# A decoder layer's feed-forward: w_up's products in 512 columns, and the norm, convolution and silu of most activations in w_down's stage

## The chip, the cores and the metric

The kernel runs on one core of a Trainium2 chip. The metric is the device time of one execution in microseconds (us); less is better. The core has five engines, each with its own instruction queue that it works through in order: TensorE (PE in the profile, its weight loads PEld), VectorE (DVE), ScalarE (ACT), GpSimd (POOL), and SyncE (SP), which here only issues DMAs. They meet through semaphores.

## What is computed

One decoder layer on 512 tokens of width 2048 in float32: a token mixer, a cross-attention, a convolutional feed-forward and a final norm. The change concerns the feed-forward alone (4096 gate and 4096 value features):

```
h = h + conv_ffn(rmsnorm(h, norm_ffn), w_up, ffn_conv, w_down)

def conv_ffn(hn, w_up, ffn_conv, w_down):
    up = causal_dwconv(hn @ w_up, ffn_conv)      # three taps along the tokens
    gate, val = jnp.split(up, 2, axis=-1)
    return (jax.nn.silu(gate) * val) @ w_down

out = rmsnorm(h, norm_final)
```

The scale of the norm that belongs to a token (`rstd`) is a factor of a whole column here, so the kernel multiplies it in after the product with w_up.

## The kernel before

**Numbers in two parts.** Matmuls take float32 operands in a rounded form. To keep precision each operand is split: `wh` is the rounded value (a cast on ACT), `wl` the rest (a subtraction on DVE). A product then needs three matmuls per k: high weights by high features, high weights by low features, low weights by high features.

**w_up's stage** (region `p_g`). Activations are made in 32 pairs j: 128 gate features and 128 value features, for all 512 tokens. The first three pairs (`plain_pair`) are plain products. The other 29 (`up_pair`) use Strassen's scheme in Winograd's form on 2x2 blocks (two halves of the 2048 input features, two halves of the tokens): seven products of 8 k each instead of eight. The token halves are 256 wide (`HT`), and the features of all seven forms lie ready in SBUF as high and low parts side by side (`xb`, `fb`). `product` splits a weight block into the two pool buffers `wh`, `wl` and runs the 24 matmuls of one product into a PSUM tile; `combine` makes the sums of weight blocks on DVE. The weight blocks of a pair come in by four DMAs of 512 KB on SP's queue, into `sraw` (four buffers) and `raw` (three). The sum a21 + a22 is made by a fifth DMA on POOL's queue, which adds while it stores. The PSUM tiles a, b, c, d hold running sums; DVE adds c's copy `s7` (in the small pool `misc`, buffer name `m0`, two buffers), and multiplies by `rstd` into `v`.

`conv_mult` follows at once: for value and gate a scaled copy on ACT and two multiply-adds on DVE (the taps), silu on ACT, gate times value on POOL, and a store of the 128 x 512 activation to DRAM (`a_d[j]`) on POOL's queue.

**w_down's stage** (region `p_d`). The 32 activations are taken in four chunks of eight. For each chunk four groups g of 512 output features follow; a group is 8 k by 4 token tiles by three matmuls of 512 columns, 96 in all. `load_acts` loads a chunk's activations from `a_d` into `m0` and splits them (`ah`, `al`), all eight behind the first group of the chunk before. `down_weights` loads two k of w_down by one DMA into `raw` and splits them into `wh` and `wl`, again two buffers each, so a split waits until PE has used up the pair of k before the last. DVE adds four finished sums to `ht` after each group. In chunk 0 each group is preceded by loads and transposes of the residual (`load_h`). Chunk 3 runs groups 2 and 3 first, then token tile by token tile with the final norm.

**What sets the order.** The scheduler of the tile framework orders each engine's instructions ahead of time, by data, buffers and priority. Weight loads, splits and combinations carry `high_priority(1000000)`. Once built, the order of each engine is fixed.

Of the kernel before, what the change touches and what calls it, by code (L numbers as in the profile page):

```python
# [17 lines left out]
P = 128  # L18
# [40 lines left out]
def decoder_kernel(ctx: ExitStack, tc: tile.TileContext, x, mem, norm_mix, w_in, dn_conv, dn_a_log, dn_dt_bias, dn_norm,  # L59
# [920 lines left out]
    NCH = 4  # L980
    a_d = [dram.tile([P, S], F32, name=f"a{j}") for j in range(32)]
    with region("p_g") as gp:
# [22 lines left out]
        def sums(k):  # L1005
            hg = sp_.tile([P, 2, S], F32, name="sraw", bufs=4)
# [7 lines left out]
            dve.tensor_tensor(v[:, 0, :], b11, b12, op=ALU.subtract)  # L1014
            dve.scalar_tensor_tensor(v[:, 1, :], v[:, 0, :], -1.0, b22, op0=ALU.mult, op1=ALU.subtract)
            dve.tensor_tensor(v[:, 2, :], b22, b12, op=ALU.subtract)
            dve.scalar_tensor_tensor(v[:, 3, :], v[:, 1, :], -1.0, b21, op0=ALU.mult, op1=ALU.subtract)
# [13 lines left out]
        def product(acc, w, of, first):  # L1031
            wh, wl = (wsp.tile([P, 8, P], F32R, name=n) for n in ("wh", "wl"))
            with tc.high_priority(1000000):
                act.copy(wh, w)  # L1034
                dve.tensor_tensor(wl, w, wh.bitcast(F32), op=ALU.subtract)  # L1035
            for k in range(8):
# [3 lines left out]
                pe.matmul(acc, wl[:, k, :], m[:, 0, :], start=False, stop=(k == 7), skip_group_check=True)  # L1040
# [6 lines left out]
        def up_pair(j):  # L1047
            quad = []
            with tc.high_priority(1000000):
                for i, (h, c) in enumerate(((0, j), (0, 32 + j), (1, 32 + j), (1, j))):  # L1050
                    r = rawp.tile([P, 8, P], F32, name="raw") if i % 2 else sp_.tile([P, 8, P], F32, name="sraw", bufs=4)
# [4 lines left out]
            a, b, c, d = (pw.tile([P, HT], F32, name=n) for n in ("sa", "sb", "sc", "sd"))  # L1056
            v, u = two("v"), two("u")
# [10 lines left out]
            s2 = combine(a11, s1, a11, ALU.add)  # L1068
            s7 = misc.tile([P, HT], F32, name="m0")
# [182 lines left out]
```

## Time and profile before

| | us |
|---|---|
| median of 3 runs | 2847.39 |
| lowest, highest | 2843.1, 2848.35 |
| profiled execution | 2842.91 |
| its span | 2841.1 |
| w_up's 29 pairs, first to last matmul | 1879.0 to 2470.4 |
| w_down, first matmul | 2471.3 |

How to read the lines. A row of the groups gives line, engine, operation, what it writes and reads, shape and count; then busy time, the mean of one in ns, the idle time before them and who ended it. A row of the timeline gives start, duration, engine, line and operation; where several like ones are merged, the duration is that of all. A matmul's duration is its latency, which overlaps with the next one's; the distance of starts is what it costs. Starts are counted from the span's beginning. The granted clock of TensorE was full in all the stretches that are shown.

### The profile page before, as it was taken

What the parts mean: (1) busy time and instruction counts of PE and PEld (TensorE: products, weight loads), DVE (VectorE), ACT (ScalarE), POOL (GpSimd) and SP (SyncE); (2) the same over time, 40 slices, a digit from 0 to 9 for tenths busy, and PEclk for the clock granted to TensorE, in tenths of its full rate; (3) what the DMA queues carried; (4) which work ended last, traced back from release to release, by engine and by line L of the source; (5) the groups of instructions that cost most, each with busy time, mean ns of one, the idle gap of its engine ahead of it and who ended that gap; (6) DMA issues with size and microseconds to landing.
All of it is one profiled execution on the core that took longest, in us unless ns stands there. A gap on an engine that the chain in (4) does not pass through costs nothing. (4 is left out here: it accounts for less than half of the span.)

```text
span 2841.1 us, 40771 instructions
## 1 busy us (share of the span) xinstructions
PE 2778.4 (98%) x15959; PEld 2402.4 (85%) x15959; DVE 1851.8 (65%) x2771; ACT 1261.4 (44%) x2099; POOL 349.8 (12%) x317
## 2 busy tenths in 40 slices
PE   7999999999999999999999999999999999999998
PEld 7788888887888877778888887789999999978886
DVE  7777787877777645434554345778888888743435
ACT  6455555545434434443223333644545455532223
POOL 3000000001011000010231110311111111100002
PEclk9999999999999999999999999999999999999999
DMA  6544444443222222223555432766666666553323
GB/s 211 137 133 138 135 133 127 134 127 93 57 67 60 54 69 67 67 71 89 159 173 161 141 119 86 230 165 139 148 139 148 139 147 139 162 172 125 120 97 112
DMA packets 528467, 354.53 MB, mean 125 GB/s; under 512 B 15345, under 2 KB 483810, under 8 KB 527634
## 3 DMA queue, kind: packets, MB, share of 16 engines
q1 hardware_dynamic: 487872, 303.74, 37.3%
q0 software_dynamic: 39760, 47.93, 7.6%
q8 instruction: 125, 2.05, 0.3%
q14 instruction: 68, 0.56, 0.1%
q10 hardware_dynamic: 642, 0.26, 0.0%
HBM read 316.74 MB, written 35.13 MB: 124 GB/s over the span
## 5 line engine op out<-in xcount | busy, mean ns | idle before, releaser
L164 DVE TENSOR_TENSOR wl<-raw,wh 128x512 fp32r<-128x512 f32 x394 | 290.6, 773 | 258.7 <-ACT wh L163 255.7
L170 PE MATMUL acc<-x,wl 128*128 128x512 f32 x1152 | 455.2, 395 | 1.1 <-DVE wl L164 1.1
L168 PE MATMUL acc<-x,wh 128*128 128x512 f32 x1152 | 455.3, 395 | 0.5 <-ACT wh L163 0.5
L169 PE MATMUL acc<-x,wh 128*128 128x512 f32 x1152 | 455.2, 395 | 0.0
L163 ACT CAST wh<-raw 128x512 fp32r<-128x512 f32 x408 | 235.7, 621 | 412.0 <-PE acc L169 208.2
L170 PEld LDWEIGHTS acc<-x,wl 128*128 128x128 f32 x1152 | 217.0, 188 | 47.0 <-DVE wl L164 2.8
L168 PEld LDWEIGHTS acc<-x,wh 128*128 128x128 f32 x1152 | 216.9, 188 | 44.2 <-issue 1.0
L169 PEld LDWEIGHTS acc<-x,wh 128*128 128x128 f32 x1152 | 216.9, 188 | 44.0 <-issue 1.7
L1034 ACT CAST wh<-sraw 128x1024 fp32r<-128x1024 f32 x87 | 91.7, 1054 | 150.0 <-PE sa L1039 93.3
L1169 DVE TENSOR_TENSOR wl<-raw,wh 128x512 fp32r<-128x512 f32 x112 | 72.4, 688 | 131.1 <-ACT wh L1168 131.0
L1168 ACT CAST wh<-raw 128x512 fp32r<-128x512 f32 x112 | 64.1, 620 | 177.6 <-PE gps L1175 171.4
L1034 ACT CAST wh<-raw 128x1024 fp32r<-128x1024 f32 x87 | 91.5, 1052 | 110.7 <-PE sd L1039 58.2
L1040 PE MATMUL sb<-fb,wl 128*128 128x256 f32 x464 | 131.4, 283 | 0.0
L1038 PE MATMUL sa<-x,wh 128*128 128x256 f32 x464 | 131.3, 283 | 0.0
L1039 PE MATMUL sa<-x,wh 128*128 128x256 f32 x464 | 131.3, 283 | 0.0
L1038 PE MATMUL sb<-fb,wh 128*128 128x256 f32 x464 | 131.3, 283 | 0.0
L1040 PE MATMUL sa<-x,wl 128*128 128x256 f32 x464 | 131.3, 283 | 0.0
L1039 PE MATMUL sb<-fb,wh 128*128 128x256 f32 x464 | 131.3, 283 | 0.0
L366 DVE TENSOR_TENSOR wl<-sm,wh 128x1024 fp32r<-128x1024 f32 x67 | 82.1, 1226 | 62.2 <-ACT wh L365 62.2
L1035 DVE TENSOR_TENSOR wl<-sraw,wh 128x1024 fp32r<-128x1024 f32 x87 | 106.3, 1222 | 19.2 <-ACT wh L1034 19.2
L1035 DVE TENSOR_TENSOR wl<-raw,wh 128x1024 fp32r<-128x1024 f32 x87 | 106.1, 1220 | 17.2 <-ACT wh L1034 17.2
L365 ACT CAST wh<-sm 128x1024 fp32r<-128x1024 f32 x67 | 70.6, 1053 | 84.8 <-PE sb L370 28.9
(584 smaller groups left out, 7595.5 us busy)
## 6 DMA issues: line engine op xcount, KB each, us to landing
raw<-in_w_in_dram SPq DMA_DIRECT2D x146, 512.0 KB, 3.8
raw<-in_w_up_dram SPq DMA_DIRECT2D x70, 512.0 KB, 4.9
raw<-in_w_down_dram SPq DMA_DIRECT2D x64, 512.0 KB, 3.8
sraw<-in_w_up_dram SPq DMA_DIRECT2D x58, 512.0 KB, 4.5
sraw<-in_w_in_dram SPq DMA_DIRECT2D x50, 512.0 KB, 3.8
raw<-in_w_o_dram SPq DMA_DIRECT2D x32, 512.0 KB, 4.1
raw<-in_w_up_dram POOLq DMA_DIRECT2D x29, 512.0 KB, 7.0
gate<-g POOLq DMA_DIRECT2D x21, 512.0 KB, 2.9
```

What stands on the lines that cost most here:

```text
L163: act.copy(wh[:, part, :], raw[:, part, :])
L164: (pool if share and s0 else dve).tensor_tensor(wl[:, part, :], raw[:, part, :], wh[:, part, :].bitcast(F32), op=ALU.subtract)
L168: pe.matmul(acc, wh[:, j, :], hs[k], start=(k == 0), stop=False)
L169: pe.matmul(acc, wh[:, j, :], ls[k], start=False, stop=False)
L170: pe.matmul(acc, wl[:, j, :], hs[k], start=False, stop=(k == nk - 1))
L366: dve.tensor_tensor(wl, w, wh.bitcast(F32), op=ALU.subtract)
L1034: act.copy(wh, w)
L1035: dve.tensor_tensor(wl, w, wh.bitcast(F32), op=ALU.subtract)
L1038: pe.matmul(acc, wh[:, k, :], m[:, 0, :], start=(first and k == 0), stop=False, skip_group_check=True)
L1039: pe.matmul(acc, wh[:, k, :], m[:, 1, :], start=False, stop=False, skip_group_check=True)
L1040: pe.matmul(acc, wl[:, k, :], m[:, 0, :], start=False, stop=(k == 7), skip_group_check=True)
L1169: dve.tensor_tensor(wl, raw[:, i, :], wh.bitcast(F32), op=ALU.subtract)
```

## The change

1. `product` writes 512 columns: high weights by high and low features side by side in one matmul of 512 columns (two halves of a PSUM tile twice as wide), then low weights by high features, 256 columns, into the first half. The two halves are added later (the folding): ACT copies one half or DVE adds `s7`, then DVE adds the halves, with `m0` as the place for it; `s7` moves to `sg`.
2. The sum a21 + a22 is made by DVE; the accumulating DMA is gone. Some signs change (in `sums` and `combine`) so that no negation is needed.
3. `up_pair` no longer multiplies by `rstd`, nor runs the convolution: it stores the raw pair `v` (128 x 1024) to DRAM, `up_d[j]`. A new function `late_act` loads it, multiplies by `rstd` on DVE and runs `conv_mult`. For pairs 3 to 7 this is asked for within w_up's stage (behind pairs 12, 15, 18, 21, 24, with one buffer `cv`), for pairs 8 to 31 in w_down's stage (two buffers `cv` and `cu`), three activations behind each of the first three groups, with the split straight from `cu`.
4. `sraw` has three buffers instead of four.

```diff
             for k in range(8):
                 m = of(k)
-                pe.matmul(acc, wh[:, k, :], m[:, 0, :], start=(first and k == 0), stop=False, skip_group_check=True)
-                pe.matmul(acc, wh[:, k, :], m[:, 1, :], start=False, stop=False, skip_group_check=True)
-                pe.matmul(acc, wl[:, k, :], m[:, 0, :], start=False, stop=(k == 7), skip_group_check=True)
+                pe.matmul(av, wh[:, k, :], m, start=(first and k == 0), stop=False, skip_group_check=True)
+                pe.matmul(av[:, 0, :], wl[:, k, :], m[:, 0, :], start=False, stop=(k == 7), skip_group_check=True)
...
-            s3 = combine(four("s3"), a11, a21, ALU.add)
-            with tc.high_priority(1000000):
-                pool.dma_start(out=a21, in_=w_up[8 * P:16 * P, (32 + j) * P:(33 + j) * P].rearrange("(k p) c -> p k c", p=P),
-                               accum_op=ALU.add)
-            s1 = a21
+            s3 = combine(four("s3"), a11, a21, ALU.subtract)
...
+            s1 = combine(a21, a21, a22, ALU.add)
+            s2 = combine(a11, s1, a11, ALU.subtract)
+            s7 = misc.tile([P, S], F32, name="sg")
...
-            dve.tensor_tensor(v[:, 1, HT:S], d, s7, op=ALU.add)
+            t = misc.tile([P, S], F32, name="m0")
+            dve.tensor_tensor(t, d, s7, op=ALU.add)
+            dve.tensor_tensor(v[:, 1, HT:S], t[:, 0:HT], t[:, HT:S], op=ALU.add)
...
-            dve.tensor_tensor(v[:, 0, HT:S], d, rstd[:, HT:S], op=ALU.mult)
-            conv_mult(j, v, u)
+            la = misc.tile([P, HT], F32, name="m0")
+            act.copy(la, d[:, HT:S])
+            dve.tensor_tensor(v[:, 0, HT:S], d[:, 0:HT], la, op=ALU.add)
+            pool.dma_start(out=up_d[j], in_=v)
...
+        def late_act(j, v, u):
+            nc.sync.dma_start(out=v, in_=up_d[j])
+            dve.tensor_tensor(v, v, rstd.unsqueeze(1).broadcast_to([P, 2, S]), op=ALU.mult)
+            conv_mult(j, v, u)
...
+            if j >= 10 and j % 3 == 0 and NS + (j - 12) // 3 < 8:
+                jl = NS + (j - 12) // 3
+                v, u = sp_.tile([P, 2, S], F32, name="cv", bufs=1), two("u")
+                late_act(jl, v, u)
+                pool.dma_start(out=a_d[jl], in_=u[:, 0, :])
...
                 down(ch, (g,))
-                if g == 0:
-                    load_acts(ch + 1)
+                for i in range(3 * g, min(3 * g + 3, 8)):
+                    load_act(8 * ch + 8 + i)
```

Where this lands on the engines is shown at three places. First PE, at the end of w_up's last product and the start of w_down (`x`, `fb` features, `sg` a tile of the residual, `gps` a sum of w_down). Before:

```order
L1038 MATMUL sd<-x_15074,wh 128x256
L1039 MATMUL sd<-x_15074,wh 128x256
L1040 MATMUL sd<-x_15074,wl 128x256
L1151 MATMUL acc<-ident,sg 128x128 x8
L1174 MATMUL gps<-wh,x_22429 128x512
L1175 MATMUL gps<-wh,x_22429 128x512
L1176 MATMUL gps<-wl,x_22429 128x512
```

And now:

```order
L1038 MATMUL sd<-x_15106,wh 128x512
L1039 MATMUL sd<-x_15106,wl 128x256
L1168 MATMUL acc<-ident,sg 128x128 x8
L1191 MATMUL gps<-wh,x_20844 128x512 x4
L1192 MATMUL gps<-wh,x_20844 128x512
L1193 MATMUL gps<-wl,x_20844 128x512
```

Two matmuls per k stand where three stood; between the stages the same eight transposes stand in both.

Second SP's queue at the same border (`raw` weights, `m` the buffer `m0` with an activation, `sg` a tile of the residual). Before:

```order
L1052 DMA raw<-in_w_up_dram 128x8x128 x2
L1159 DMA raw<-in_w_down_dram 128x2x512
L1138 DMA m_22427<-a_14575 128x512
L1159 DMA raw<-in_w_down_dram 128x2x512
L1138 DMA m_22432<-a_14576 128x512
L1159 DMA raw<-in_w_down_dram 128x2x512
L1138 DMA m_22437<-a_14577 128x512
```

And now:

```order
L1051 DMA raw<-in_w_up_dram 128x8x128
L1176 DMA raw<-in_w_down_dram 128x2x512
L1165 DMA sg<-h_0_12718 128x512
L1176 DMA raw<-in_w_down_dram 128x2x512 x2
L1165 DMA sg<-h_1_12719 128x512
L1176 DMA raw<-in_w_down_dram 128x2x512
L1151 DMA m_20842<-a_14607 128x512
L1176 DMA raw<-in_w_down_dram 128x2x512
L1151 DMA m_20847<-a_14608 128x512
```

The first activation's load stood behind the first load of w_down and now stands behind the fourth.

Third DVE in w_down's chunk 0, about the second group (`wl` a weight split, `ah` the split of an activation, `ht` the addition of four sums, `cv` the norm multiply, `cu` a convolution step). Before:

```order
L1185 TENSOR_TENSOR ht_22421<-gps,ht_22421 128x512 x4
L1169 TENSOR_TENSOR wl<-raw,wh 128x512 x2
L146 TENSOR_TENSOR ah_22652<-m_22650,ah_22652 128x512
L146 TENSOR_TENSOR ah_22657<-m_22655,ah_22657 128x512
L146 TENSOR_TENSOR ah_22662<-m_22660,ah_22662 128x512
L146 TENSOR_TENSOR ah_22667<-m_22665,ah_22667 128x512
L1169 TENSOR_TENSOR wl<-raw,wh 128x512 x2
L146 TENSOR_TENSOR ah_22672<-m_22670,ah_22672 128x512
L1169 TENSOR_TENSOR wl<-raw,wh 128x512 x4
L1185 TENSOR_TENSOR ht_22422<-gps,ht_22422 128x512 x4
```

And now, between two additions of sums:

```order
L1186 TENSOR_TENSOR wl<-raw,wh 128x512 x2
L146 TENSOR_TENSOR ah_21092<-cu,ah_21092 128x512
L1115 SCALAR_TENSOR_TENSOR cu<-cv,ffcw,cu 128x511 x2
L1115 SCALAR_TENSOR_TENSOR cu<-cv,ffcw,cu 128x510 x2
L1106 TENSOR_TENSOR cv<-cv,rstd 128x1024
L1186 TENSOR_TENSOR wl<-raw,wh 128x512 x2
L146 TENSOR_TENSOR ah_21275<-cu,ah_21275 128x512
L1115 SCALAR_TENSOR_TENSOR cu<-cv,ffcw,cu 128x511 x2
L1115 SCALAR_TENSOR_TENSOR cu<-cv,ffcw,cu 128x510 x2
L1106 TENSOR_TENSOR cv<-cv,rstd 128x1024
L1186 TENSOR_TENSOR wl<-raw,wh 128x512 x2
```

About one whole activation (a split, four convolution steps and a norm multiply) now stands between one pair of weight splits and the next; chunk 1's and chunk 2's sixteen activations follow one another in this way through five groups, and chunk 3's come after a group without any.

More of the change, by code (lines that the diff above doesn't have):

```diff
@@ L980, in decoder_kernel @@
     NCH = 4
+    up_d = [dram.tile([P, 2, S], F32, name=f"up{j}") for j in range(32)]
     a_d = [dram.tile([P, S], F32, name=f"a{j}") for j in range(32)]
@@ L1005, in sums @@
         def sums(k):
-            hg = sp_.tile([P, 2, S], F32, name="sraw", bufs=4)
+            hg = sp_.tile([P, 2, S], F32, name="sraw", bufs=3)
             for j in range(2):
@@ L1013, in sums @@
             v = four("s3").rearrange("p a b -> p (a b)").rearrange("p (i c) -> p i c", i=4)
[L1014 to L1017, printed above, removed]
+            for i, (p_, q_) in enumerate(((b12, b11), (b22, v[:, 0, :]), (b22, b12), (b21, v[:, 1, :]))):
+                dve.tensor_tensor(v[:, i, :], p_, q_, op=ALU.subtract)
             act.copy(fb[k][:, 0, :, :], v)
@@ L1050, in up_pair @@
                 for i, (h, c) in enumerate(((0, j), (0, 32 + j), (1, 32 + j), (1, j))):
-                    r = rawp.tile([P, 8, P], F32, name="raw") if i % 2 else sp_.tile([P, 8, P], F32, name="sraw", bufs=4)
+                    r = rawp.tile([P, 8, P], F32, name="raw") if i % 2 else sp_.tile([P, 8, P], F32, name="sraw", bufs=3)
                     nc.sync.dma_start(out=r, in_=w_up[h * 8 * P:(h + 1) * 8 * P, c * P:(c + 1) * P]
@@ L1055, in up_pair @@
             a11, a21, a22, a12 = quad
[L1056 to L1062 removed]
+            a, b, c, d = (pw.tile([P, S], F32, name=n) for n in ("sa", "sb", "sc", "sd"))
+            v = two("v")
+            s3 = combine(four("s3"), a11, a21, ALU.subtract)
             product(a, a11, B11, True)
@@ L1108, in conv_mult @@
             pool.tensor_tensor(u[:, 0, :], u[:, 0, :], u[:, 1, :], op=ALU.mult)
-            pool.dma_start(out=a_d[j], in_=u[:, 0, :])
         NS = 3
@@ L1120, in decoder_kernel @@
                     for _ in range(2):
-                        pe.matmul(pw.tile([P, HT], F32, name=n), xb[0][:, 0, 0:P], xb[0][:, 0, 0:HT], start=True, stop=True)
+                        pe.matmul(pw.tile([P, S], F32, name=n), xb[0][:, 0, 0:P], xb[0][:, 0, :], start=True, stop=True)
             up_pair(j)
+            if j >= 10 and j % 3 == 0 and NS + (j - 12) // 3 < 8:
[3 more added lines that the diff above has]
+                pool.dma_start(out=a_d[jl], in_=u[:, 0, :])
         psum.close()
@@ L1132, in decoder_kernel, with load_act @@
         pool.dma_start(out=gfb, in_=norm_final.partition_broadcast(P))
-        def load_acts(ch):
-            for i in range(8):
-                j = ch * 8 + i
+        def load_act(j):
+            ch, i = j // 8, j % 8
+            if ch == 0:
                 raw = misc.tile([P, S], F32, name="m0")
                 nc.sync.dma_start(out=raw, in_=a_d[j])
-                if ch % 2 == 0:
-                    ah[j], al[j] = split_slot(i)
-                else:
-                    both = gp.tile([P, 2, S], F32R, name=f"ah{i}", bufs=1)
-                    ah[j], al[j] = both[:, 0, :], both[:, 1, :]
-                split(ah[j], al[j], raw)
+            else:
+                v, u = (gp.tile([P, 2, S], F32, name=n, bufs=2) for n in ("cv", "cu"))
+                late_act(j, v, u)
+                raw = u[:, 0, :]
+            if ch % 2 == 0:
+                ah[j], al[j] = split_slot(i)
+            else:
+                both = gp.tile([P, 2, S], F32R, name=f"ah{i}", bufs=1)
+                ah[j], al[j] = both[:, 0, :], both[:, 1, :]
+            split(ah[j], al[j], raw)
         def load_h(m):
@@ L1185, in down @@
                     dve.tensor_tensor(ht[g][:, t, :], accs[t], ht[g][:, t, :], op=ALU.add)
-        load_acts(0)
+        for j in range(8):
+            load_act(j)
         for ch in range(NCH - 1):
```

15 lines of the change are left out of this document (9 added, 6 removed).

## The prediction

> **What bounds the kernel now.** I read the page's engine table first, then windows of the stages that the change touches, then the groups of instructions there, then the timeline at the places where engines meet.
>
> ```profile
> span 2841.1 us, 40771 instructions
> ...
> PE 2778.4 (98%) x15959; PEld 2402.4 (85%) x15959; DVE 1851.8 (65%) x2771; ACT 1261.4 (44%) x2099; POOL 349.8 (12%) x317
> ```
>
> The profiled execution took 2842.91 us (1.8 us around its span), 4.5 us under the median of the three runs, 2847.39 us. TensorE (PE) is the bound over the whole span. But its "busy" is a modelled union, so I go by how many matmuls fit into a stretch. Columns: each engine's busy time with its instruction count, then granted clock, DMA share, GB/s.
>
> ```profile
> 2000.00:2203.00 203.00, 203.00 (x1682) 201.99 (x1681) 175.92 (x191) 101.61 (x130) 36.66 (x30) 1.00 0.64 143
> 300.00:498.00 198.00, 198.00 (x1123) 171.76 (x1122) 156.88 (x171) 103.17 (x130) 5.34 (x10) 1.00 0.47 133
> ...
> 2496.10:2610.80 114.70, 112.03 (x513) 92.42 (x512) 46.85 (x75) 36.30 (x64) 0.00 (x0) 1.00 0.46 147
> ```
>
> Row 1 is the w_up stage (29 pairs of 168 matmuls): 203/1682 = 120.7 ns each, 20.28 us per pair. Row 2 is the gates' stage of the same kernel, which already has the form that the change brings (512 and 256 columns in turn, lines 370 and 371): 198/1123 = 176.3 ns, 112 matmuls to a pair, 19.75 us. Row 3 is the w_down stage from its first to its sixth group of sums: VectorE (DVE) works 46.85 of 114.7 us. That idle half is where the change puts work.
>
> ```profile
> L1169 DVE TENSOR_TENSOR wl<-raw,wh 128x512 fp32r<-128x512 f32 x112 | 72.4, 688 | 131.1 <-ACT wh L1168 131.0
> L1168 ACT CAST wh<-raw 128x512 fp32r<-128x512 f32 x112 | 64.1, 620 | 177.6 <-PE gps L1175 171.4
> ...
> L1044 DVE TENSOR_TENSOR raw<-raw,sraw 128x1024 f32<-128x1024 f32 x29 | 62.8, 2166 | 1.0
> ...
> L1044 DVE TENSOR_TENSOR sraw<-raw,sraw 128x1024 f32<-128x1024 f32 x28 | 34.1, 1219 | 0.0
> ...
> L1107 ACT ACTIVATE u<-u 128x512 f32<-128x512 f32 x29 | 18.4, 635 | 3.9 <-DVE u L1106 0.5
> ```
>
> Columns: count, busy us, mean ns of one, idle time before and what ended it. In w_down DVE's weight split waits 131 us for ScalarE's (ACT's) cast, and the cast 171 us for PE to free a weight buffer: PE leads. And the same addition (L1044) takes 1219 ns in one place and 2166 ns in the other. The timeline says why; DVE first, then GpSimd (POOL):
>
> ```profile
> 2131.95 0.75 DVE L1106 SCALAR_TENSOR_TENSOR u<-v,ffcw,u 128x510 f32<-128x510 f32 x1
> 2132.62 1.22 DVE L1035 TENSOR_TENSOR wl<-raw,wh 128x1024 fp32r<-128x1024 f32 x1
> 2133.87 2.20 DVE L1044 TENSOR_TENSOR raw<-raw,sraw 128x1024 f32<-128x1024 f32 x1
> 2135.99 1.21 DVE L1035 TENSOR_TENSOR wl<-raw,wh 128x1024 fp32r<-128x1024 f32 x1
> 2137.17 0.43 DVE L1075 TENSOR_TENSOR v<-sa,rstd 128x256 f32<-128x256 f32 x1
> ...
> 2133.51 1.48 POOL L1108 TENSOR_TENSOR u<-u 128x512 f32<-128x512 f32 x1 [1.95 <-ACT u L1107]
> ```
>
> POOL's multiply ends at 2134.99; the addition that DVE began under it ends 1.08 us later, as if it had only then begun. So one multiply of POOL costs a busy DVE 2166 - 1219 = 0.95 us. Starts also give DVE's true step: 0.67 us per convolution step (2131.95 to 2132.62), 1.18 us per 1024-wide operation (2135.99 to 2137.17).
>
> [...]
>
> **The change part by part.**
>
> First, the matmuls. Each k of a product had three of 256 columns and gets one of 512 and one of 256. By rows 1 and 2: (20.28 - 19.75) x 29 pairs = **-15 us**.
>
> ```profile
> 2470.39 0.28 PE L1040 MATMUL sd<-x,wl 128*128 128x256 f32 x1
> 2470.51 1.04 PE L1151 MATMUL acc<-ident,sg 128*128 128x128 f32 x8
> 2471.32 0.47 PE L1174 MATMUL gps<-wh,x 128*128 128x512 f32 x1
> ```
>
> The bounds: the last w_up matmul and its successor start 0.12 us apart, 168 x 0.12 = 20.16 us, so w_up's pairs hold 0.12 us of small waits. If they come on top of 19.75 (w_up has two weight buffers where the gates have three), the gain is -12; if not, -15.
>
> Second, DVE in the w_up stage. Per pair it has 7 splits and 4 combinations (the sum a21+a22, until now an accumulating DMA, is the fourth): 11 x 1.18 = 13.0 us, and the folding, priced by the gates' rows:
>
> ```profile
> L412 DVE TENSOR_TENSOR m<-sd,sg 128x512 f32<-128x512 f32 x25 | 17.1, 685 | 0.3 <-PE sd L371 0.3
> ...
> L374 DVE TENSOR_TENSOR g<-sa,m 128x256 f32<-128x256 f32 x25 | 10.5, 418 | 0.0
> ```
>
> 2 x 0.69 + 4 x 0.42 = 3.1, so 16.1 of 19.75 us: hidden. The sign edits in sums cost nothing. On the queues, POOL loses 29 accumulating transfers and gets 29 stores of up, both 512 KB; a store has until the next pair's fold to leave v, two thirds of a pair. But five activations stay in this stage, and the scheduler puts them into five successive pairs. Each adds 1.18 (norm) + 4 x 0.67 (convolution) + 0.95 (POOL's lock) = 4.8 us: 20.9 against 19.75, 1.15 x 5 = **+6 us**. Bounds: +1 if the lock doesn't bite; +11 if the norm multiply, which waits for a load into the single buffer cv, comes a microsecond late each time, since the next weight split is queued behind it on DVE and PE waits for that.
>
> Third, the start of w_down. The folding now lives in m0, the two buffers that also receive the first activations. SP's issues before:
>
> ```profile
> 2447.01 0.37 SPq L1159 DMA_DIRECT2D raw<-in_w_down_dram  x1
> 2448.17 0.34 SPq L1138 DMA_DIRECT2D m<-a  x1
> ...
> 2470.21 0.38 SPq L1159 DMA_DIRECT2D raw<-in_w_down_dram  x1
> ```
>
> And the DMA issues with their size and time to landing:
>
> ```profile
> sraw<-in_w_up_dram SPq DMA_DIRECT2D x58, 512.0 KB, 4.5
> sraw<-in_w_in_dram SPq DMA_DIRECT2D x50, 512.0 KB, 3.8
> ...
> m<-a SPq DMA_DIRECT2D x32, 256.0 KB, 3.8
> ```
>
> The first activation was asked for at 2448.17, 23 us before it was used at 2471.32. In the new order it stands behind the fourth load of w_down, which went out at 2470.21 (it waits for the first one's split). Then 0.4 for the issue, 3.8 for the landing, 0.62 for ACT's cast: 2475.0 instead of 2471.3, **+4 us**. Bounds: 0, if transposes and weights fill it; +9, if the next activations, each waiting for one of two m0 buffers, are late too.
>
> Fourth, the activations in w_down. 24 of 32 are now made there. In the stretch of row 3 the new order gives DVE 40 weight splits, 20 additions of sums, 15 splits of activations, 64 convolution steps and 17 norm multiplies.
>
> ```profile
> 2496.11 2.48 DVE L1185 TENSOR_TENSOR ht<-gps,ht 128x512 f32<-128x512 f32 x4
> 2498.50 1.28 DVE L1169 TENSOR_TENSOR wl<-raw,wh 128x512 fp32r<-128x512 f32 x2
> 2499.70 1.29 DVE L146 TENSOR_TENSOR ah<-m,ah 128x512 fp32r<-128x512 f32 x2
> ...
> 2610.79 2.73 DVE L1185 TENSOR_TENSOR ht<-gps,ht 128x512 f32<-128x512 f32 x4 [1.68 <-PE gps L1176]
> ```
>
> Four additions take 2.39 us and two splits 1.20 us from start to start, 0.60 each: 40 x 0.60 + 20 x 0.60 + 15 x 0.60 + 64 x 0.67 + 17 x 1.18 = 108 us, and 16 multiplies of POOL by 0.95 make it 123 where PE needed 2610.8 - 2496.1 = 114.7. DVE takes instructions in order and the weight splits stand between the activations' steps; two weight buffers let it run one pair ahead at most. So DVE becomes the bound: +9. The chain of an activation (DVE, ACT's silu, POOL, ACT's cast, DVE) adds waits: none at best (L412 above waits 0.3 us in 25), and at worst 0.64 + 1.48 + 0.62 (silu, multiply, cast) less the 2.4 us that a norm multiply and two splits cover, 0.36 x 16 = 6. I take 2, nearer the row: **+11 us**, bounds 0 (no lock) and +15.
>
> Last, chunk 3's eight activations fall among 24 weight splits and 16 additions: 49 us and 7 x 0.95, 56 of PE's 65 (three groups). Hidden on the whole, bunched in places: **+1**, bounds 0 and +6. The new transfers (24 loads of 512 KB in some 130 us, 97 GB/s on top of row 3's 147) I cost at nothing, since the chip moves as much in other slices (8 of the 40 exceed 150 GB/s, one shows 230):
>
> ```profile
> GB/s 211 137 133 138 135 133 127 134 127 93 57 67 60 54 69 67 67 71 89 159 173 161 141 119 86 230 165 139 148 139 148 139 147 139 162 172 125 120 97 112
> ```
>
> If they land late, the norm multiply waits and the fourth term grows.
>
> Sum: -15 + 6 + 4 + 11 + 1 = **+7 us**: 2849.9 on the profiled execution's basis, and on the median 2847.4 + 7 = **2854**.
>
> **The rivals.**
>
> Faster: DVE never becomes the bound in w_down, since the lock costs it little (POOL's multiply falling on sums read from PSUM, or on waits that are there anyway). It decides at (114.7 - 108)/16 = 0.4 us per multiply: under that, the fourth term is 0, the second 1, the last 0: -15 + 1 + 4 = -10, 2837. Against it stand the 29 additions of 2166 ns; for it, that those all stand at one and the same place of a pair.
>
> Slower by more: w_up's sraw falls from four buffers to three, so a22 of the next pair is loaded only when the old a11 is free, one and a half products (of 19.75/7 = 2.82 us) before it is added to a21, some 4.2 us. At 3.8 us (sraw in the gates, three buffers too) it is in time; beyond 4.2 (w_up shows 4.5) the addition blocks DVE ahead of a weight split. If it comes 0.5 us late (an estimate: 4.5 and an issue against 4.2) in each of 28 pairs, that is 14 more: 2868. DMA traffic becomes that of the gates, which speaks against it.
>
> [...]
>
> **How the numbers follow.** A measurement of this kernel can tell about 0.2% (5.7 us) from no change. The forecast, 0 to +14 (2847 to 2861), has 0.53, a little over half of it slower by that much; the faster rival 0.22 (mostly beyond -5.7); the buffer rival 0.17; the columns rule 0.03; the rest, to both sides, 0.05. That makes faster 0.20, the same 0.30, slower 0.50. The range takes in the faster rival and the buffer rival: 2836 to 2872.
>
> **What would show it.** Right: in w_up, a pair every 19.8 us outside five pairs that take about 21; a gap of some 4 us ahead of the first w_down matmul; groups of w_down at 24 to 26 us in chunks 0 and 1 with DVE near 95% busy there, PE waiting for wl, and POOL's multiply ahead of long DVE rows. Wrong: pairs at 20.2 or more (first term), DVE waiting for the load of cv or a22, w_down groups at the old pace (fourth term).

## The result, and the profile after

The changed kernel takes 2872.44 us (median of 6 runs, 2862.57 to 2877.83) against 2847.36 us of the kernel before (6 runs, 2841.56 to 2848.35) on the same chip: ratio 1.0093, 95% interval 1.0078 to 1.0107, **25 us slower**. The forecast was 2854, slower by 7, in a range up to 2872: the sign was right, the size was not.

The head of the page of the changed kernel:

```profile
span 2868.9 us, 37624 instructions
...
PE 2775.8 (97%) x14335; PEld 2324.8 (81%) x14335; DVE 1916.4 (67%) x2858; ACT 1288.4 (45%) x2157; POOL 308.5 (11%) x293
```

TensorE's busy time stays (2778.4 before) and the span grows by 27.8 us: PE now waits. The stages, in windows of the changed kernel (busy time with instruction count for PE, PEld, DVE, ACT, POOL; then granted clock, DMA share, GB/s):

```profile
2040.00:2243.00 203.00, 203.00 (x1153) 176.42 (x1152) 160.60 (x174) 96.56 (x124) 5.87 (x11) 1.00 0.44 133
300.00:498.00 198.00, 198.00 (x1144) 174.68 (x1144) 160.43 (x176) 104.05 (x132) 5.32 (x10) 1.00 0.48 136
1913.60:2017.10 103.50, 87.59 (x450) 74.27 (x449) 78.68 (x91) 44.09 (x60) 10.13 (x12) 0.92 0.44 135
2472.30:2510.30 38.00, 30.07 (x123) 23.17 (x121) 21.62 (x32) 16.82 (x30) 5.74 (x4) 0.87 0.73 249
2510.30:2634.60 124.30, 116.49 (x522) 94.96 (x521) 116.66 (x154) 66.31 (x115) 26.42 (x16) 0.99 0.53 172
```

Row 1 is w_up without late activations: 203/1153 = 176.1 ns per matmul, 19.72 us per pair, as forecast. Row 3 is the four pairs that hold late activations: 450 matmuls in 103.5 us where row 1 would need 79.2; PE stands idle for 15.9 us of it, at a mean clock of 0.92. Row 4 is the start of w_down, row 5 its second to sixth group of sums: VectorE is busy 94% (before, 41%). Row 2 is the gates' stage, which the change doesn't touch; the end of the document comes back to it.

Measured in the two traces from the first matmul of each stage (us):

| | before | after | difference | forecast |
|---|---|---|---|---|
| up to w_up's first Strassen pair | 1879.0 | 1871.0 | -8.0 | 0 |
| w_up, 29 pairs at the steady step | 20.30 each | 19.79 each | -14.8 | -15 |
| w_up, five late activations on top | | 24.72, 25.60, 27.84, 25.38, 20.08 | +24.7 | +6 |
| last w_up to first w_down matmul | 0.9 | 5.8 | +4.9 | +4 |
| first group of sums | 24.6 | 32.2 | +7.6 | (in the above) |
| groups 2 to 6 | 116.8 | 124.4 | +7.6 | +11 |
| groups 7 to 10 | 87.2 | 90.8 | +3.6 | +1 |
| behind the last matmul | 11.1 | 13.1 | +2.0 | 0 |

The first row is no work of the change (see the end). Without it the stages that the change touches lost 35.6 us in this execution; the 8 us that it gave back are luck.

**The five late activations** are most of it. Waits in the window of row 3 (who waited for what: us in total, times, longest):

```profile
ACT u L1111 <- DMA a<-u: 19.6, 4, 6.0
...
PEld sd L1038 <- ACT wh L1033: 15.4, 4, 4.8
PE sd L1038 <- DVE m L1077: 14.3, 4, 4.6
DVE cv L1106 <- DMA cv<-up: 6.0, 4, 1.7
...
PE sb L1039 <- DVE wl L1034: 1.5, 3, 0.6
```

And the timeline of one of these pairs (start, duration, instruction; in brackets the idle time before it and what ended it):

```profile
1922.57 0.34 SPq L1105 DMA_DIRECT2D cv<-up  x1
...
1924.58 1.39 POOL L1117 TENSOR_TENSOR u<-u 128x512 f32<-128x512 f32 x1 [7.10 <-ACT u L1116]
...
1926.27 0.58 POOL L1135 DMA_DIRECT2D a<-u  x1 [0.30 <-POOL u L1117]
1926.31 1.23 DVE L1106 TENSOR_TENSOR cv<-cv,rstd 128x1024 f32<-128x1024 f32 x1 [1.49 <-DMA cv<-up]
...
1930.46 0.72 ACT L1111 ACTIVATE u<-cv,ffcw 128x512 f32<-128x512 f32 x1 [3.88 <-DMA a<-u]
1931.09 1.03 ACT L1033 CAST wh<-raw 128x1024 fp32r<-128x1024 f32 x1
...
1932.15 1.23 DVE L1034 TENSOR_TENSOR wl<-raw,wh 128x1024 fp32r<-128x1024 f32 x1 [2.01 <-ACT wh L1033]
```

There is one buffer u. The store of one activation out of u is issued at 1926.27, and until it lands, at 1930.4, the next activation's convolution (L1111) can't write u. It stands on ScalarE ahead of a weight's rounding (L1033), so the weight comes 4 us late, its split on VectorE too, and behind the split stands the folding addition L1077, which frees the PSUM tile that PE writes next. PE's 15.9 idle us are 14.3 behind that chain and 1.5 behind the wait for cv's load, which the prediction had named. And a wait of PE costs more than its own length. The same place in windows of one or two us:

```profile
1932.00:1934.00 2.00, 0.00 (x0) 0.00 (x0) 1.84 (x3) 1.68 (x3) 0.00 (x0) 1.00 0.09 27
1934.00:1935.00 1.00, 0.87 (x3) 0.81 (x4) 1.00 (x2) 0.00 (x0) 0.00 (x0) 0.60 0.28 68
1935.00:1937.00 2.00, 2.00 (x8) 1.71 (x7) 2.00 (x3) 0.00 (x0) 0.00 (x0) 0.50 0.82 228
1937.00:1938.00 1.00, 1.00 (x5) 0.85 (x5) 1.00 (x3) 0.00 (x0) 0.00 (x0) 0.69 0.00 1
1938.00:1939.00 1.00, 1.00 (x8) 0.86 (x7) 0.18 (x1) 0.36 (x1) 0.00 (x0) 1.00 0.00 0
```

After 2.55 us without a matmul the granted clock is 0.50, for 3.4 us in this stretch of the trace: in the timeline a pair of matmuls (512 and 256 columns) then starts every 0.64 us, and every 0.35 us ahead of the wait. In the four pairs 17.1 us ran at half clock. So row 3's loss of 24.3 us is 15.9 of waiting and 8.4 of slow matmuls (87.6 busy where 79.2 were needed).

**The start of w_down**, in windows of 5 us:

```profile
2475.00:2480.00 5.00, 1.93 (x5) 1.54 (x6) 0.69 (x1) 1.10 (x2) 1.06 (x2) 0.69 0.87 265
2480.00:2485.00 5.00, 3.56 (x9) 2.26 (x7) 0.00 (x0) 0.52 (x1) 0.00 (x0) 0.63 1.02 417
2485.00:2490.00 5.00, 4.11 (x17) 3.43 (x18) 2.60 (x3) 2.28 (x5) 0.00 (x0) 0.72 0.83 297
```

The DMA engines are full (share 1.02, 417 GB/s): the last norm's weights gfb (1 MB), the first late activation (0.5 MB), weights and residual land together, and the second activation's load, issued at 2474.90, lands 9.6 us later in place of 3.8. PE stands idle for part of the time, and the granted clock is 0.63 to 0.72 in these windows.

### The profile page after: what moved, and what is told of

Same layout as the page of the kernel before. It is cut to its first block, busy times and chain, and to the rows that moved or that the text cites. A ratio compares the mean times of both kernels' runs of the same rounds, so it can differ in the third digit from the quotient of the medians.

```text
span 2868.9 us, 37624 instructions
## 1 busy us (share of the span) xinstructions
PE 2775.8 (97%) x14335; PEld 2324.8 (81%) x14335; DVE 1916.4 (67%) x2858; ACT 1288.4 (45%) x2157; POOL 308.5 (11%) x293
## 5 line engine op out<-in xcount | busy, mean ns | idle before, releaser
L169 PEld LDWEIGHTS acc<-x,wh 128*128 128x128 f32 x1152 | 217.7, 189 | 44.3 <-issue 2.2
L1038 PE MATMUL sa<-x,wh 128*128 128x512 f32 x464 | 166.7, 399 | 0.0
L1038 PE MATMUL sb<-fb,wh 128*128 128x512 f32 x464 | 166.4, 398 | 0.0
L1033 ACT CAST wh<-sraw 128x1024 fp32r<-128x1024 f32 x87 | 91.4, 1050 | 124.0 <-PE sa L1038 66.7
L1033 ACT CAST wh<-raw 128x1024 fp32r<-128x1024 f32 x87 | 91.4, 1050 | 112.7 <-PE sd L1038 37.9
L1034 DVE TENSOR_TENSOR wl<-sraw,wh 128x1024 fp32r<-128x1024 f32 x87 | 106.6, 1225 | 52.4 <-ACT wh L1033 52.0
L1191 PE MATMUL gps<-wh,x 128*128 128x512 f32 x256 | 101.3, 399 | 6.0 <-ACT x L145 3.7
L1038 PEld LDWEIGHTS sa<-x,wh 128*128 128x128 f32 x464 | 87.6, 189 | 21.9 <-ACT sb L1059 0.3
```

The costliest lines, as they stand in the source:

```text
L169: pe.matmul(acc, wh[:, j, :], ls[k], start=False, stop=False)
L1038: pe.matmul(av, wh[:, k, :], m, start=(first and k == 0), stop=False, skip_group_check=True)
L1191: pe.matmul(acc, ah[j][:, ts], wh, start=(k == 0), stop=False)
```

## The experiments

Each was timed against the kernel before on the same chip. All kernels, stage by stage in their profiled execution (us; "start" is the gap and the first group; the six groups behind the tenth take 130.5 in all):

| | w_up | start | groups 2-10 | median time | ratio to before, 95% |
|---|---|---|---|---|---|
| before | 591.4 | 25.5 | 204.0 | 2847.4 | 1 |
| after | 601.3 | 38.0 | 215.2 | 2872.4 | 1.0093 [1.0078, 1.0107] |
| e1_spread | 577.6 | 35.3 | 215.1 | 2851.0 | 1.0022 [1.0013, 1.0031] |
| e2_start | 602.5 | 35.8 | 219.1 | 2878.8 | 1.0115 [1.0100, 1.0130] |
| e3_no_gate | 602.4 | 36.0 | 202.4 | 2863.5 | 1.0060 [1.0044, 1.0077] |
| e4_inline | 611.6 | 32.4 | 202.2 | 2866.4 | 1.0071 [1.0056, 1.0086] |
| e5_norm | 607.4 | 35.9 | 217.7 | 2882.3 | 1.0137 [1.0122, 1.0152] |
| e6_gfb | 576.4 | 34.9 | 214.8 | 2851.1 | 1.0023 [1.0013, 1.0033] |
| e7_half | 625.7 | 35.8 | 214.1 | 2895.3 | 1.0173 [1.0152, 1.0195] |
| e8_inline4 | 595.1 | 31.7 | 201.5 | 2852.0 | 1.0028 [1.0016, 1.0040] |
| e9_norm4 | 584.4 | 35.8 | 218.6 | 2862.1 | 1.0063 [1.0046, 1.0080] |
| e10_held | 576.8 | 30.5 | 219.6 | 2850.6 | 1.0024 [1.0014, 1.0033] |
| e11_gate_down | 590.4 | 33.2 | 211.2 | 2858.5 | 1.0051 [1.0036, 1.0065] |
| e12_gate_start | 592.5 | 28.6 | 215.7 | 2855.6 | 1.0039 [1.0026, 1.0052] |
| e13_dve_gate | 576.7 | 37.9 | 202.7 | **2832.4** | **0.9966 [0.9951, 0.9981]** |
| e14_dve_start | 577.0 | 33.0 | 205.3 | 2836.6 | 0.9970 [0.9957, 0.9983] |

**e1_spread: the chain of five, or a pair that is too full?**

```diff
-        for j in range(32):
+        rest = list(range(8, 32))
+        order = [0, 1, 2]
+        for i in range(5):
+            order += [3 + i] + rest[4 * i:4 * i + 4]
+        order += rest[20:]
+        for j in order:
...
-            if j >= 10 and j % 3 == 0 and NS + (j - 12) // 3 < 8:
-                jl = NS + (j - 12) // 3
+            if 8 <= j < 28 and j % 4 == 2:
+                jl = NS + (j - 10) // 4
```

> The order of the pairs in w_up is changed so that the source pairs of the five late activations (3 to 7) stand five pairs apart (0 1 2, 3, 8 9 10 11, 4, 12 ...); the arithmetic is the same. Theory A (the loss in w_up is the chain of the five: the next one's convolution, on ScalarE and ahead of a weight's rounding, waits until the store of the one before has left the only buffer u, 19.6 us of waits in four pairs; its load into the only cv adds 6 us on VectorE): the pairs that hold an activation fall from 24.7 us (mean of the five) to at most 21.0, the w_up stage from 601 to 577-583 us, the time from 2872 to 2848-2855. Theory B (a pair with an activation is too full for VectorE and ScalarE whatever stands around it): such pairs stay at 24 to 26 us at their new places, the stage at 597-602, the time at 2866-2876.

Theory A. The pairs with an activation take 20.0 to 20.4 us, w_up 577.6, and the time falls by 21 us. Three rows that stand together in the list of all waits of its w_up:

```profile
ACT wh L1033 <- ACT u L1116: 3.8, 5, 0.8
PEld sd L1039 <- DVE wl L1034: 3.0, 7, 0.6
DVE raw L1043 <- DMA sraw<-in_w_up_dram: 2.3, 5, 0.6
```

The list has no wait for a<-u and none for cv<-up any more, and PE's weight loads wait 3.0 us for a split, in seven pieces. One late activation that stands alone costs 0.2 to 0.6 us, less than the 1.15 that the prediction's volume gave. e1 removes both waits at once; that u's store weighs more than cv's load is read from the waits, and was not tried by itself.

**e2_start, e6_gfb, e10_held: the start of w_down.** e2 gives the last pair's temporaries another buffer:

```diff
+            cv = sp_.tile([P, 2, S], F32, name="cv", bufs=1) if j == 31 else None
+            spare = lambda i: misc.tile([P, S], F32, name="m0") if cv is None else cv[:, i % 2, :]
...
-            la = misc.tile([P, HT], F32, name="m0")
+            la = spare(0)[:, 0:HT]
```

> Only the last pair of w_up takes its four temporaries from the buffer cv (free by then) instead of the two buffers m0, so that w_down's first activations can be loaded into m0 a pair earlier. Theory A (the start is late because m0 is held until the last folding additions): the gap between the last w_up matmul and the first w_down matmul falls from 5.8 to at most 1.5 us and the first group from 32.2 to 24-28 us; the time falls by 8 to 13 us, to 2859-2864. Theory B (the first group is long because of the new work in it, the first activations of chunk 1 among it, or because of the transfers, 250 GB/s in it): what the border gains the first group gives back, gap and group stay at 36-38 us together, time 2869-2875.

Nearer theory B: gap 3.6 and group 32.2, the groups behind took 4 us more, and the time came out above both. A wait of VectorE at the start shows why:

```profile
DVE cv L1108 <- DMA cv<-up: 11.7, 1, 11.7
```

With m0 free, the loads of the first late activations (2 x 0.5 MB) and gfb all start within a microsecond, at 2485 us, and VectorE stands 11.7 us behind the first of them, with the weights' splits queued behind it. e6 is e1 with gfb's load written at the end of w_down's second chunk:

```diff
-        pool.dma_start(out=gfb, in_=norm_final.partition_broadcast(P))
...
                 down(ch, (g,))
+                if ch == 1 and g == 3:
+                    pool.dma_start(out=gfb, in_=norm_final.partition_broadcast(P))
```

> As e1_spread, but the load of the last norm's weights (gfb, 1 MB, needed only in the last chunk) is issued at the end of w_down's second chunk instead of at w_down's start. Theory A (the start of w_down is late because transfers fill the DMA engines there: share 1.02 at 417 GB/s between 2480 and 2485 us of the changed kernel, an activation's load took 9.6 us instead of 3.9): border and first group, 5.4 + 29.9 us, fall by 5 to 9 us, time 2842-2847. Theory B (it is late because the first load waits for the buffer m0, which the last pair's folding additions hold): the border stays at 5 to 6, the first group falls by at most 2, time 2849-2852.

It tells nothing on the theories: the load depends on nothing, and the scheduler issued it at 2458.3 all the same, right behind w_up. e10 therefore makes the loads depend on something (with e2's edit, on e1):

```diff
-        pool.dma_start(out=gfb, in_=norm_final.partition_broadcast(P))
...
+                if ch == 0 and g == 1:
+                    act.copy(gfb[:, 0:1], ht[0][:, 0, 0:1])
+                    pool.dma_start(out=gfb, in_=norm_final.partition_broadcast(P))
...
+            if after is not None:
+                act.copy(v[:, 0, 0:1], after)
             nc.sync.dma_start(out=v, in_=up_d[j])
...
-                late_act(j, v, u)
+                late_act(j, v, u, ht[0][:, 0, 384:385] if j < 10 else None)
```

> As e1_spread, with w_down's start freed of two things at once: the last pair's temporaries are in cv, not in m0 (as e2_start), and the loads of gfb (1 MB) and of the first two late activations (2 x 0.5 MB) are made to wait until the first group has been added (a copy of one column into their buffers ahead of the load; e6_gfb changed the line but not the moment, the load was issued at w_down's start all the same). Theory A (border and first group, 5.4 + 29.9 us, are loads of activations that wait first for m0 and then for the full DMA engines): border at most 1.5, first group 23-26, together 35.3 to 24-27; the groups behind it at most 3 us longer; time 2840-2845. Theory B (what is held comes late: the activations of chunk 1 miss their place): the first group gains, groups 2 to 5 lose as much, time 2848-2855.

Both in part: gap and first group fall from 35.3 to 30.5, and groups 2 to 10 give 4.5 back, the second alone 4.5 (29.5 us in place of 25.0). The two held loads are issued together, 25 us behind w_down's first matmul (2 and 5 us behind it in e1); that the groups pay for just this was not tried.

**e3_no_gate: GpSimd's product in w_down.** The products of the 24 activations there are left out.

```diff
-            pool.tensor_tensor(u[:, 0, :], u[:, 0, :], u[:, 1, :], op=ALU.mult)
+            if mult:
+                pool.tensor_tensor(u[:, 0, :], u[:, 0, :], u[:, 1, :], op=ALU.mult)
...
-                late_act(j, v, u)
+                late_act(j, v, u, mult=False)
                 raw = u[:, 0, :]
```

> The multiplication of gate and value on GpSimd is left out for the 24 activations made in w_down (the output is then another one; load, norm, convolution and silu stay). Theory A (the loss in w_down's groups 1 to 9 comes from VectorE standing still while GpSimd multiplies, 0.95 us each, as the prediction had it): the groups 1 to 9, 216 us together, fall by 8 to 11 us, the time to 2861-2865. Theory B (it comes from the volume of VectorE's own work and the chain load, norm, convolution, silu): they fall by 0 to 3 us, time 2868-2875.

Theory A, somewhat above its size: groups 2 to 10 fall by 12.8 us, to less than before the change.

**e4_inline: was the move needed?** Norm, convolution, silu and product of all pairs stay in w_up.

```diff
-            pool.dma_start(out=up_d[j], in_=v)
+            u = two("u")
+            dve.tensor_tensor(v, v, rstd.unsqueeze(1).broadcast_to([P, 2, S]), op=ALU.mult)
+            conv_mult(j, v, u)
+            pool.dma_start(out=a_d[j], in_=u[:, 0, :])
...
-            if ch == 0:
+            if True:
```

> The wide product alone: the norm multiplication, convolution, silu and product of every pair stay in w_up behind its folding additions, and w_down loads finished activations, as before. Theory A (VectorE then bounds the pairs: 15.45 us of work in a pair without an activation, +1.2 for the norm, +4 x 0.74 for the convolution, +0.95 for the stop by GpSimd's product = 20.6): a pair takes 20.3 to 21.2 us, the w_up stage 590-618 us, w_down as before (358-363 us), the time 2835-2862. Theory B (the engines absorb it, the move was not needed): pairs of 19.8 to 19.9, stage 577-580, time 2824-2834.

Theory A: 21.05 us a pair (the time, 2866, is above its range). The wide product alone loses too; w_down is then as before but for its start. There the gap stays at 6.0, but the first group falls from 32.2 to 26.4: of its +7.6 us, some 5.7 came with the late activations, their loads or their work.

**e5_norm, e7_half, e8_inline4, e9_norm4: how much may a pair hold?** e5 moves only the norm back into w_up, on e1:

```diff
+            dve.tensor_tensor(v, v, rstd.unsqueeze(1).broadcast_to([P, 2, S]), op=ALU.mult)
             pool.dma_start(out=up_d[j], in_=v)
...
             nc.sync.dma_start(out=v, in_=up_d[j])
-            dve.tensor_tensor(v, v, rstd.unsqueeze(1).broadcast_to([P, 2, S]), op=ALU.mult)
```

> As e1_spread, but the multiplication by rstd of every pair stays in w_up, behind its folding additions (one VectorE instruction of 1.2 us per pair), and the late activations have only convolution, silu and product left. Theory A (w_down's groups 1 to 9 are bound by VectorE, its work and its stops by GpSimd: leaving the stops out, 24 x 0.95 = 23 us, took 15 us off them): 24 x 1.13 = 27 us less of VectorE there take about as much, w_down falls from 375 to 359-364 us; in w_up 15.45 + 1.2 = 16.7 us of VectorE stay under the pair's 19.79 and the stage stays at 577-581; time 2851 to 2834-2842. Theory B (only the stops and the chain of dependent steps count, not the volume): w_down stays at 370-375, time 2846-2852.

and e7 half of the convolution as well (the value's half, channels 32 + j, by the edit; the expectation calls it the gate's):

```diff
-            pool.dma_start(out=up_d[j], in_=v)
+            u = two("u")
+            dve.tensor_tensor(u[:, 0, :], v[:, 0, :], rstd, op=ALU.mult)
+            dve.tensor_tensor(v[:, 1, :], v[:, 1, :], rstd, op=ALU.mult)
+            conv(u[:, 1, :], v[:, 1, :], 32 + j)
+            pool.dma_start(out=up_d[j], in_=u)
```

> As e5_norm, but the gate's half of the convolution too stays in w_up (two VectorE instructions of 0.74 us and one of ScalarE per pair more); the late activations have the value's half, silu and product left. Theory A (VectorE's volume): 24 x 2.4 = 58 us less of VectorE in w_down than in e1_spread, groups 1 to 9 come down to 21.8 to 23 each but for the four with transposes, w_down 357-362 us; w_up at 15.45 + 1.2 + 1.45 = 18.1 us of VectorE per pair stays PE's, 577-583; time 2832-2841. Rival (18.1 us in pieces that wait for one another do not fit beside the weights' splits, as 20.6 in e4_inline did not and cost 21.03): pairs of 20.0 to 20.4, the stage 584-592, time 2840-2852.

Both missed. With 1.2 us more of VectorE a pair rose by 1.4 us, to a median of 21.2, though by volume VectorE had 3 us to spare. VectorE's waits between 2000 and 2450 us of e5:

```profile
DVE wl L1034 <- ACT wh L1033: 37.1, 60, 1.6
DVE raw L1043 <- DMA sraw<-in_w_up_dram: 30.9, 19, 2.4
```

and of e1:

```profile
DVE wl L1034 <- ACT wh L1033: 77.1, 97, 1.6
DVE raw L1043 <- DMA sraw<-in_w_up_dram: 2.0, 4, 0.6
```

The load of a22 starts when VectorE has released one of three sraw buffers; the norm multiply delays the release, the load comes late, VectorE stands at the addition and the next release is late too. This is the prediction's buffer rival: asleep in the changed kernel, awake as soon as VectorE gets more to do. Two more runs test it with sraw's fourth buffer back (in neither is there a cv in this stage), e8 on e4, e9 on a form with the norm in every pair:

```diff
-            hg = sp_.tile([P, 2, S], F32, name="sraw", bufs=3)
+            hg = sp_.tile([P, 2, S], F32, name="sraw", bufs=4)
```

> As e4_inline (wide product alone, norm and convolution of every pair in w_up), but with four buffers sraw instead of three for the weights' quarters, as before the change. Theory A (the pairs of 21.03 us in e4_inline are VectorE's volume, 20.6 us worked out): pairs stay at 20.8 to 21.1, the stage at 606-612, time 2862-2868. Theory B (with three buffers the load of a22 is issued only when VectorE has finished with a11, so every piece of work that VectorE gets ahead of that delays the next load, and VectorE then waits for it: 37 us of waits for sraw's loads in e5_norm's w_up against 3.8 in e1_spread's): pairs fall to 19.8-20.4, the stage to 577-594, time 2832-2850.

```diff
+            dve.tensor_tensor(v, v, rstd.unsqueeze(1).broadcast_to([P, 2, S]), op=ALU.mult)
+            if j < 8:
+                u = two("u")
+                conv_mult(j, v, u)
+                pool.dma_start(out=a_d[j], in_=u[:, 0, :])
+            else:
+                pool.dma_start(out=up_d[j], in_=v)
```

> Four buffers sraw again; every pair of w_up multiplies by rstd as in e5_norm; pairs 3 to 7 also do convolution, silu and product at once (there is no late activation in w_up and no buffer cv there); the 24 others are left to w_down without the norm. Theory B of e8_inline4: pairs of 19.8 to 20.0 from the eighth on, the stage 577-583; w_down, with 27 us less of VectorE's work, 364-372 us; time 2835-2845. Theory A of e8_inline4 (volume, order of VectorE's queue): pairs stay at 20.4 to 21.4 as in e5_norm, the stage at 595-607, time 2862-2880.

For e9 theory B held in w_up: 19.93 a pair with the norm in it, where e5 had 21.2. Its groups 2 to 10 did not get shorter without the norm (218.6), in e5 as little, and so the time missed; why was not followed up. For e8 neither held whole: the buffer was worth 0.6 of the 1.25 us, and a pair takes 20.41, just above theory B's range. VectorE is busy in e8

```profile
2000.00:2450.00 450.00, 441.74 (x2465) 376.40 (x2464) 444.93 (x485) 244.40 (x331) 52.14 (x44) 1.00 0.39 115
```

for 444.9 of 450 us, the stops by GpSimd among them. e11 takes from it only GpSimd's product:

```diff
-            conv_mult(j, v, u)
-            pool.dma_start(out=a_d[j], in_=u[:, 0, :])
+            conv_mult(j, v, u, j < 8)
+            if j < 8:
+                pool.dma_start(out=a_d[j], in_=u[:, 0, :])
+            else:
+                pool.dma_start(out=up_d[j], in_=u)
...
+                nc.sync.dma_start(out=u, in_=up_d[j])
                 raw = u[:, 0, :]
+                pool.tensor_tensor(raw, raw, u[:, 1, :], op=ALU.mult)
```

> As e8_inline4 (wide product, four sraw, norm, convolution and silu in w_up), but for the pairs 8 to 31 only the product of gate and value, which GpSimd makes and for which VectorE stands still 0.95 us, is left to w_down: both halves are stored, loaded there and multiplied. Theory A (at 20.4 us a pair e8_inline4 is bound by VectorE's volume with its stops, 445 of 450 us busy; in w_down VectorE has time over once norm and convolution are not there): pairs from the eighth on fall to 19.8-19.9, the stage from 595 to 578-585, w_down stays at 358-362, time 2852 to 2835-2845. Theory B (the pairs' 20.4 us come from the order of the dependent pieces, not from the stops): pairs stay at 20.2 to 20.5, time 2848-2855.

and e12 adds to that a free start (gfb held as in e10, the last pair's temporaries in sraw):

```diff
+            last = sp_.tile([P, 8, P], F32, name="sraw", bufs=4).rearrange("p (i a) b -> p i (a b)", i=2) if j == 31 else None
+            spare = lambda i: misc.tile([P, S], F32, name="m0") if last is None else last[:, i % 2, :]
```

> As e11_gate_down, with the start of w_down freed: the last pair's temporaries in a buffer sraw, which no later load needs, in place of m0, and gfb's load (1 MB) behind the first group. Theory A (m0, then the full DMA engines, as for e10_held): border from 5.7 to at most 2, first group from 26 to 24-26, nothing later lost, since no late convolution needs an early load; 5 to 7 us under e11_gate_down, 2829-2840. Theory B (the start is given by something else): within 2 us of e11_gate_down.

In w_up e11 is theory B: pairs of 20.3, 0.1 less, although VectorE's share falls:

```profile
2000.00:2450.00 450.00, 440.53 (x2490) 380.47 (x2489) 431.05 (x490) 246.54 (x332) 14.12 (x24) 1.00 0.46 129
```

So it is not VectorE's volume alone that sets e8's pairs; what else does is open. Groups 2 to 10 pay 10 us for products and larger loads, and the time misses both ranges. e12 is between its two theories: its start gains 4.6 us and groups 2 to 10 give 4.5 back.

**e13_dve_gate, e14_dve_start: the product on VectorE.** On e1, VectorE makes w_down's products itself; e14 adds e2's edit and holds gfb's load as in e10.

```diff
-            pool.tensor_tensor(u[:, 0, :], u[:, 0, :], u[:, 1, :], op=ALU.mult)
+            by.tensor_tensor(u[:, 0, :], u[:, 0, :], u[:, 1, :], op=ALU.mult)
...
-                late_act(j, v, u)
+                late_act(j, v, u, dve)
                 raw = u[:, 0, :]
```

> As e1_spread, but the products of gate and value of the 24 activations made in w_down are made by VectorE (0.6 us each) and not by GpSimd (which stops VectorE 0.95 us each). Theory A (the stops cost by their length, like any other work of VectorE there): 24 x 0.35 = 8 us less of VectorE in groups 1 to 9, which give about 4-6 us; w_down 375 to 368-372, time 2851 to 2844-2848. Theory B (the stops fall on the splits of the weights, for which PE waits, and the way over GpSimd and back lengthens the chain to the next group's operand): w_down falls by 8 to 13 us, to 362-367, time 2838-2843. Theory C (GpSimd's product costs nothing, e3_no_gate gained by the missing step alone): w_down rises by 2 to 6 us, time 2852-2858.

> As e13_dve_gate, with the last pair's temporaries in cv in place of m0, and gfb's load behind the first group; the late activations' loads stay where they were. Theory A (m0 and the full DMA engines make w_down's start late): border at most 4, first group 24-27, together 35 to 28-31, nothing lost later; 4 to 7 us under e13_dve_gate, 2833-2842. Theory B (the transfers come in another order but the same loads must land before the first and second group): the second group or the third takes back what the first gains, within 2 us of e13_dve_gate.

Theory B for e13: groups 2 to 10 fall by 12.4 us, to 202.7, as if the products were not there, and at **2832.4 us** (below the range forecast) the kernel beats both, by 0.3% against before. The start took 2.6 us longer than in e1, cause open. Of the median's fall of 18.6 us against e1 the two profiled executions show 11.6 (2838.9 against 2850.5); the rest is not accounted for. Groups 2 to 6 (which hold 16 products), of e1, of e3 and of e13:

```profile
2490.20:2614.60 124.40, 116.49 (x524) 94.96 (x523) 117.38 (x154) 66.30 (x115) 26.48 (x16) 0.99 0.55 172
```

```profile
2515.40:2630.00 114.60, 113.41 (x522) 93.60 (x519) 106.55 (x154) 64.16 (x112) 0.00 (x0) 1.00 0.58 185
```

```profile
2490.70:2606.20 115.50, 114.29 (x523) 94.12 (x522) 112.98 (x167) 65.68 (x114) 0.00 (x0) 1.00 0.57 182
```

The same 154 instructions of VectorE take 117.4 us beside GpSimd's products and 106.6 without them: 10.8/16 = 0.68 us for each. Made by VectorE itself each takes a step of 0.60 us, hardly less (e13's row holds 16 of them, and for it five other steps of the activations fewer and two additions of sums more). And VectorE is 98% busy in e13 without holding PE up. So volume explains little of e1: its 117.4 us are 1.9 more than e13's whole stretch, and it took 8.9 longer. The rest is waits. ScalarE waits for GpSimd's result in these groups, with weights' roundings behind it, and PE for VectorE's additions of sums:

```profile
ACT x L145 <- POOL cu L1117: 7.1, 7, 1.8
...
PEld gps L1196 <- DVE ht L1207: 4.5, 2, 2.8
...
ACT ah L145 <- POOL cu L1117: 2.8, 6, 0.6
```

e13 removes the stops and the way over GpSimd together; which of the two weighs more was not tried.

e14 against e13 is theory B in kind: the start gains 4.9 us, the second group loses 3.3, and the intervals don't tell the two apart (e14's median is 4.2 us higher).

## Why the prediction was wrong, point by point

- **Matmuls, -15: right.** 20.30 to 19.79 us a pair, -14.8. The row of the gates' stage was the right price. No run shows the "columns rule" that has a chance of 0.03 in the prediction; what the runs showed is 3 x 120.7 = 362 ns per k in w_up before and 2 x 176.1 = 352 ns after.
- **Late activations in w_up, +6: the step that failed, +24.7.** The prediction priced them as volume (20.9 us of VectorE against 19.75) and bounded them, at +11, by cv's load. It checked that a store "has until the next pair's fold to leave v", and made no such check for u, which has one copy as well and which each late activation stores from. Five activations in successive pairs are a chain: multiply, store, landing, and only then the next convolution, on ScalarE ahead of a weight. e1 shows it: apart, they cost 0.2 to 0.6 us each, also less than the volume said.
- **The half clock: missing altogether.** PE's waits were priced at their own length. 8.4 of the 24.3 us in the four pairs, and at most 5 us at w_down's start (10.2 us at half clock there, PE idle in part of them), are slow matmuls after the wait.
- **Start of w_down, +4: mechanism right, mis-sized.** The gap grew by 4.9, as worked out from the later issue. The first group's +7.6 was a bound there ("the next activations late too"), and they are late not only by m0 but where the DMA engines are full (417 GB/s), which the fourth term costed at nothing from the page's slices of 71 us; within 5 us the transfers do collide. The first group also makes two of the 24 late activations (products at 2498.40 and 2508.26), which this term left out; "The change" has them begin with the second. With m0 free and loads held, e10 and e12 still take 30.5 and 28.6 us where the kernel before took 25.5: that rest is open.
- **VectorE as the bound in w_down, +11: near in size, +7.6, but not by its mechanism.** VectorE was 94% busy, as forecast (its own numbers, 123 against 114.7, give +8 and not the +9 that it wrote). The stop, which the prediction calls the lock, was 0.68 us per product in place of 0.95; the runs show how long it is, and not what makes it. But e13 puts as many products on VectorE itself, is 98% busy and loses nothing, so it is the stops with the way over GpSimd, and hardly the volume, that cost. That the size came out near is in part luck.
- **Chunk 3, +1: +3.6**, by the same products, in groups 9 and 10 (23.0 and 24.0 us; 21.8 each in e3 and e13).
- **Behind the last matmul, +2.0:** not predicted, the same in all kernels with the wide product (12.7 to 13.2); its cause is open.
- **The buffer rival** did not happen in the changed kernel (19.79 a pair, 2 us of waits for sraw in e1), but e5 and e9 show it to be real: the slack was smaller than VectorE's next microsecond.

## What to carry to other kernels

When work is moved out of line, follow each single-copy buffer that it passes through from its write to the landing of its store, and ask which instruction on which in-order engine stands behind the first one that must wait for it; and make sure that a scheduler that fills idle time can't line up what was meant to be spread, here by the order of the pairs. In the changed kernel's w_up and w_down the half clock came with waits of TensorE of 2.33 us and more: price such a wait at its own length and, as a risk, half of a 3.41 us stretch on top (1.7 us, an estimate from these stretches). An idle engine that stops a busy one (0.68 us per product in e1) is no free help: this kernel was faster (2832.4 us in e13, 2851.0 in e1) with the same product on the engine that was then 98% full.

## What the runs showed of the hardware

**The clock after a wait.** In w_up and w_down of the changed kernel the granted clock is either 1 or 0.5, and 0.5 comes in stretches of 3.41 or 6.83 us, seven in all. Each begins within a wait of PE of 2.33 us or more (2.55 us in the windows above) or up to 1.4 us behind its end. Waits under 2 us (the longest 1.71 us) left the clock alone, and so did one of 2.53 us in w_down before: how long the wait is does not decide it alone.

**The stop by GpSimd.** Of 22 products in w_down's groups 2 to 10 of the changed kernel, 18 came with a VectorE instruction longer than others of its line, 13.2 us in all. It stops GpSimd too: 18 products took 1.30 to 1.60 us, and four 2.3 to 2.6. Three of these four began in the last 0.26 us of a norm multiply, and two weight splits passed before the convolution step that was then stopped:

```profile
2600.45 1.21 DVE L1106 TENSOR_TENSOR cv<-cv,rstd 128x1024 f32<-128x1024 f32 x1
2601.40 2.62 POOL L1117 TENSOR_TENSOR cu<-cu 128x512 f32<-128x512 f32 x1 [4.01 <-ACT cu L1116]
2601.59 1.28 DVE L1186 TENSOR_TENSOR wl<-raw,wh 128x512 fp32r<-128x512 f32 x2
2602.79 2.44 DVE L1115 SCALAR_TENSOR_TENSOR cu<-cv,ffcw,cu 128x511 f32<-128x511 f32 x2
2604.05 0.62 ACT L145 CAST x<-cu 128x512 fp32r<-128x512 f32 x1 [0.95 <-POOL cu L1117]
```

A product that began at the same point of a norm multiply, at 2586.15, but with four additions of sums from PSUM behind it took 1.39 us, and the additions (2.48 us for four) were no longer than before the change.

**Two paces of the same matmuls.** The gates' stage is the same code in all kernels. In the profile before it ran 1123 matmuls in 198 us (300 to 498 us), in the profile after 1144, both at clock 1.00; the whole stage took 496.9 and 488.0 us. That is the -8 us in the table's first row, and it is no gain of the change: in the profiles of all 14 experiments the stage took 496.8. Single matmuls show a regular step of 117 and 230 ns in the faster pace and one that wanders (113 to 120, 233 to 241) in the slower. w_up showed the slower pace in nearly all pairs (19.79) and the faster in a few (19.42 to 19.46). What decides between them is not settled; it is worth 2% of such a stage, as much as the change was meant to move in w_up.
